# Branch B's output product in a conv-encoder step: three of four tile pairs as seven block products

## The chip, the cores and the metric

The kernel runs on one core of one Trainium2 chip. The metric is device time in microseconds (us), the median of the runs shown. One core has a matrix engine (PE, with its weight loads as PEld), a vector engine (DVE), a scalar engine (ACT), GpSimd (POOL) and SyncE (SP); the last three issue DMAs.

## The reference, cut to what matters

One layer of a streaming encoder on 576 token columns (512 of a prompt, 64 of a running stream), model width 1024, feed-forward width 2816:

```python
x = x + 0.5 * swiglu_ffn(rms_norm(x, ffn1_norm), ffn1_w_gate_up, ffn1_w_down)
h = rms_norm(x, mix_norm)
p = h @ w_in
...
y_a = (a_b * a_conv) @ w_a_out
...
b_act = jax.nn.silu(layer_norm(b_conv + conv_b_bias, conv_b_ln_g, conv_b_ln_b))
y_b = b_act @ w_b_out
merged = jax.nn.sigmoid(gate_a) * y_a + jax.nn.sigmoid(gate_b) * y_b
x = x + merged @ w_out
x = x + 0.5 * swiglu_ffn(rms_norm(x, ffn2_norm), ffn2_w_gate_up, ffn2_w_down)
```

A final norm and the convolutions' history rows follow. All data are float32. The change is in `y_b = b_act @ w_b_out` and in where `x` lies around it.

## The kernel before

**Layout.** Features lie on the 128 partitions and tokens along the row, so an activation is eight tiles of 128 x 576. The two halves of a tile's row (288 columns each) are two matmuls. The residual x lies in eight fixed tiles `X[j]` in SBUF.

**Products in parts.** Each weight block and each activation is split in a high part, rounded to the matmul's reduced float32, and the low part that is left; a product is high x high + high x low + low x high. A *plain* output tile (`product`, L430, with `mm`, L391) takes 8 row blocks of weights x 3 parts x 2 halves = 48 matmuls of 288 columns, in two weight *units* of four row blocks (24 matmuls each).

**Pairs in block form.** Most of the two feed-forwards' gate and up tiles go as `pair` (L773): two output tiles by two halves of the features by two halves of the tokens make a 2 x 2 block product, done as seven block products of sums instead of eight. Each block is 4 row blocks x 3 parts = 12 matmuls of 288 columns. The sums of weights (`s1` to `s4`) are made by DVE from four raw weight blocks; the sums of activations are four combinations per pair of tiles, made by `Forms.combine` (L570) with four half-width DVE operations and two ACT casts, and completed by `Forms.split` (L581) with two DVE subtractions. The seven results lie in PSUM and are combined by half-width DVE operations, after each block those that its result permits (`steps`).

**The weight stream** (`Stream`, L195) prepares units in one fixed order. A raw block (512 x 128, 256 KB) is loaded on SP's queue into one of 6 buffers, its high part is cast on ACT (`begin`, L257), and its low part is made in one of two ways: "dma" (ACT writes the negated high part, and a DMA issued by POOL accumulates the raw block onto it) or "dve" (`end`, L273, a subtraction on DVE). In a pair, sums are of the second kind, the blocks 1, 5 and 7, whose weights are raw blocks, of the first. Plain mixer units are all "dma". When PE's unit n is asked for (`get`, L298), `lead` (L287) first completes units up to n + `ahead` - 1, makes the sums of units up to n + `ahead` + 1, and begins units up to n + `ahead`; `ahead` is 6 (`AHEAD_UNITS`). Each unit has a home, the pool of its two buffers: "u" (8 buffers), "g" (8, shared with convolution tiles and branch B's gates) or "act" (44, shared with the split activations). Mixer units alternate between "u" and "act".

**Order of the work.** Every engine executes its instructions in the order in which the program writes them (`Ordered`, L71), so an ACT cast written behind an instruction that waits also waits. What `product` leaves to do with its result is written behind the next product's matmuls (`behind`, `take`, L421), and small DVE pieces queued in `work` are taken between products (`fill`, L417) by a planned cost.

**The stage around the change** (L1083 to L1141): eight rounds of branch A's gate `("p", 5, j)` and output product `("ya", j)`, whose gated results `M[j]` lie in four "act" and four "w" buffers; the layer norm's and the activation's pieces for branch B (`swish`, L1029), which give the eight split operands `BA`; eight tiles of branch B's gate `("p", 6, j)`; eight plain tiles of branch B's product, each with a scaling by the gate `SGB[j]`, an addition to `M[j]` and a split into `MS[j]`; and eight tiles of the output product, whose results are added to `X[j]`.

```python
for j in range(KT):
    ps = product(("yb", j), BA)
    dve.tensor_tensor(halves(SGB[j]), ps, halves(SGB[j]), op=ALU.mult)
    dve.tensor_tensor(M[j], M[j], SGB[j], op=ALU.add)
    MS.append(split(M[j]))
```

Of the kernel before, what the change touches and what calls it, by code (L numbers as in the profile page):

```python
# [1 line left out]

# [5 lines left out]
F32 = mybir.dt.float32  # L8
# [98 lines left out]
def tile_encoder_step(  # L107
# [19 lines left out]
    tmp = ctx.enter_context(tc.tile_pool(name="tmp", bufs=6))  # L127
    rpool = ctx.enter_context(tc.tile_pool(name="rpool", bufs=1))
    mmps = ctx.enter_context(tc.tile_pool(name="mmps", bufs=4, space=bass.MemoryType.PSUM))

# [6 lines left out]
    def atile(dt=F32, n=T):  # L137
        return act.tile([P, T], dt, tag="act", name=nm("act"))[:, :n]
# [56 lines left out]
    class Stream:  # L195
# [9 lines left out]

        def raw(self, w, row0, k, col0):
            ap = w[0, row0 : row0 + k * P, col0 : col0 + P].rearrange("(k p) n -> p k n", p=P)
            self.raws.append((ap, k))
            self.last.append({})
            return len(self.raws) - 1  # L210
# [97 lines left out]
    def home(other):  # L308

        homes[0] += 1  # L310
        return ("u", other)[homes[0] % 2]

    def plan_tile(name, w, row0, ks, col0, other, home_of=None, low="dma"):
        plan[name] = []
        for k in ks:
            r = ws.raw(w, row0, k, col0)
            plan[name].append(ws.unit(r, k, home_of or home(other), low))
            row0 += k * P
# [6 lines left out]
    def plan_pair(f, gu, i):  # L325

        a21, a22, a11, a12 = (
            ws.raw(gu, h * KU * P, KU, gu_col(part, i)) for part in "ug" for h in range(2)  # L330
        )
        s1, s2, s3, s4 = (f"{f}{i}s{n}" for n in range(1, 5))
        plan[f, "s", i] = [
            ws.unit(src, KU, home("g"), low, sums)
            for src, low, sums in (
                (a11, "dma", ((s1, (a21, a22)),)),
                (s2, "dve", ((s2, (s1, a11)),)),
                (s1, "dve", ()),
                (s3, "dve", ((s3, (a11, a21)),)),
                (a12, "dma", ()),  # L340
                (s4, "dve", ((s4, (s2, a12)),)),
                (a22, "dma", ()),
            )
        ]
# [24 lines left out]

    def plan_mixer(name, w, col):  # L370
        plan_tile(name, w, 0, (KU, KU), col, "act")

# [6 lines left out]
    for j in range(KT):  # L379
        plan_mixer(("p", 5, j), w_in, 5 * D + j * P)  # L380
        plan_mixer(("ya", j), w_a_out, j * P)
    for j in range(KT):
        plan_mixer(("p", 6, j), w_in, 6 * D + j * P)
    for j in range(KT):
        plan_mixer(("yb", j), w_b_out, j * P)
    for j in IN_TURN:
        plan_mixer(("o", j), w_out, j * P)
    plan_ffn("f2", ffn2_gu, ffn2_dn)
# [15 lines left out]
    def chunks(name):  # L404

        got = []
        for n in plan[name]:
            w = ws.get(n)
            got += [(w, kk) for kk in range(ws.units[n][1])]
        return got  # L410


# [145 lines left out]
    class Forms:  # L558

        def __init__(self, r_g):
            self.r_g, self.b, self.t, self.parts = r_g, {}, {}, {}
# [166 lines left out]
    def ffn(f, xg, sums, finish, forms, R=None, todo=()):  # L730
# [42 lines left out]
        def pair(i, hs, last):  # L773
# [21 lines left out]
            for n, xs in enumerate(bs):  # L795
                w = ws.get(plan[f, "s", i][n])
                q.append(bank()[:, :H])
                for k in range(KU):
                    (whi, wlo), (xh, xl) = w, xs[k]
                    for m, (l, r) in enumerate(((whi, xh), (whi, xl), (wlo, xh))):  # L800
                        pe.matmul(
                            q[n], l[:, k, :], r, start=k == m == 0, stop=k == KU - 1 and m == 2
                        )
                if n > 0:
                    steps[n - 1]()
                if rest:
                    rest.pop(0)()
# [197 lines left out]
    def b_of(j):  # L1005
# [9 lines left out]
        return then  # L1015

    for j in range(KT):
        for b, of in ((1, c_of), (2, cv_of), (0, b_of)):
            product(("p", b, j), xg, of(j))

    M, SGB, BA = [], [], []

# [6 lines left out]
    def swish(i, RL, sig={}):  # L1029
# [13 lines left out]
        if 0 <= j < KT:  # L1043
            BA[j] = (BA[j], low(sig[j], BA[j]))

    def ga_of(j):
# [5 lines left out]
    def ya_of(j):  # L1052
        def then(ps):
            m = atile() if j < 4 else wtile(n=T)
            dve.tensor_tensor(halves(m), ps, halves(gates.pop(j)), op=ALU.mult)
            M.append(m)
        return then
# [35 lines left out]
    while stage[0] < 4:  # L1093
        while work:
            work.pop(0)()
        advance()
    work.extend((lambda i=i: swish(i, RL)) for i in range(KT + 2))

# [11 lines left out]
    while work:  # L1110
        work.pop(0)()
    take()

    MS = []
    for j in range(KT):
        ps = product(("yb", j), BA)
        dve.tensor_tensor(halves(SGB[j]), ps, halves(SGB[j]), op=ALU.mult)
        dve.tensor_tensor(M[j], M[j], SGB[j], op=ALU.add)
        MS.append(split(M[j]))

    ss = Sum()
    xg = [None] * KT
    forms = Forms(R_N2)
    table(AF.Abs_reciprocal_sqrt)
    for n, j in enumerate(IN_TURN):
        ps = product(("o", j), MS)
        dve.tensor_tensor(halves(X[j]), ps, halves(X[j]), op=ALU.add)
        xg[j] = split_scaled(X[j], par(j, R_N2))
# [127 lines left out]
```

## Time and profile before

| | |
|---|---|
| median of 3 runs | 1299.93 us (1299.71 to 1300.36) |
| the profiled execution | 1300.08 us, its span 1298.3 us |
| matmuls | 9754, mean granted clock 0.998 |
| branch A's rounds, last output tile ends | 750.96 us from the span's start |
| branch B's gate product | 750.96 to 800.88 us |
| branch B's output product | 800.88 to 850.80 us |
| the mixer's output product | 850.80 to 900.72 us |

A row of a timeline gives start, length, engine, source line, operation, tiles written and read, shapes and count, and in brackets the engine's idle time before it and what ended it. As helpers record every operation, all rows bear line L83: what tells them apart is the tile names. "act", "u", "g" and "w" are buffer pools, "mm" is PSUM, "raw" an unsplit weight block. PE's rows overlap by the drain of each matmul, so the distance between two starts, and not a length, is what a matmul costs. A bracketed busy share is an average over stages; what a stage is worth is read from its own rows.

### The profile page before, as it was taken

Reading aid. Unit: us, or ns where it says so; the run is one execution under the profiler, and the core shown is the slowest. Engines: PE = TensorE matmul, PEld = TensorE weight load, DVE = VectorE, ACT = ScalarE, POOL = GpSimd, SP = SyncE. Lnnn points to the kernel's source line nnn. Section 1 sums busy time; section 2 is a strip of 40 time slices with the busy share of each in tenths; the row PEclk is TensorE's granted clock in tenths of the full one; section 3 lists DMA queues with packets and bytes.
Section 4 is the critical chain, followed back from the end, with each engine's and each line's share of the span. In section 5 each row is a group of like instructions: output and inputs, shape, how many; then the busy total and the mean of one; then the engine's idle time right before and its main releaser. Section 6 shows DMA issues by size and latency. Waiting matters only on the chain.

```text
span 1298.3 us, 25689 instructions
## 1 busy us (share of the span) xinstructions
PE 1286.2 (99%) x9754; PEld 1283.6 (99%) x9754; DVE 892.1 (69%) x1469; ACT 768.7 (59%) x1362; POOL 380.7 (29%) x481
## 2 busy tenths in 40 slices
PE   9999999999999999999999999999999999999997
PEld 9999999999999999999999999999999999999996
DVE  6848758748945999888885160336967848847955
ACT  7746646645677654555444674467665655654664
POOL 0042332232233454333321322222142242241231
PEclk9999999999999999999999999999999999999999
DMA  7397786896698898778875978776688697796784
GB/s 219 79 196 159 157 185 155 164 196 143 151 199 180 168 212 175 169 166 177 168 168 128 197 158 174 164 157 142 139 174 175 144 194 160 155 211 133 161 176 108
DMA packets 287516, 215.39 MB, mean 166 GB/s; under 512 B 15520, under 2 KB 250016, under 8 KB 287392
## 3 DMA queue, kind: packets, MB, share of 16 engines
q0 software_dynamic: 59184, 97.28, 45.7%
q1 hardware_dynamic: 226336, 115.49, 31.4%
q8 instruction: 77, 1.26, 0.4%
q10 hardware_dynamic: 1872, 0.97, 0.3%
q14 instruction: 47, 0.39, 0.1%
HBM read 113.81 MB, written 2.62 MB: 90 GB/s over the span
## 4 chain that ended last, share of the span: by engine, by line
PE 94%; issue 2%; DVE 2%; DMA 1%; ACT 1%; POOL 0%; DVEq 0%; POOLq 0%; ACTq 0%
PE mm L83 94%; DVE tmp L83 1%; DMA u<-raw 0%; DVE g L83 0%; ACT tmp L83 0%; DMA act<-raw 0%; DMA raw<-in_ffn_w_gate_up_dram 0%; DVE x L83 0%; ACT act L83 0%; DVE acc L83 0%; ACT r L83 0%; DVE act L83 0%; ACT w L83 0%; ACT L83 0%; DVEq L1246 0%
## 5 line engine op out<-in xcount | busy, mean ns | idle before, releaser
L83 PE MATMUL mm<-act,u 128*128 128x288 f32 x4686 | 661.1, 294 | 1.2 <-DMA u<-raw 1.2
L83 PEld LDWEIGHTS mm<-act,u 128*128 128x128 f32 x4686 | 631.1, 188 | 1.7 <-DMA u<-raw 1.7
L83 PE MATMUL mm<-act,g 128*128 128x288 f32 x2778 | 399.7, 294 | 0.5 <-DMA g<-raw 0.4
L83 PEld LDWEIGHTS mm<-act,g 128*128 128x128 f32 x2778 | 378.1, 188 | 0.9 <-DMA g<-raw 0.6
L83 PE MATMUL mm<-act,act 128*128 128x288 f32 (+2 forms) x2244 | 306.7, 293 | 0.2 <-DMA act<-raw 0.2
L83 PEld LDWEIGHTS mm<-act,act 128*128 128x128 f32 x2244 | 297.6, 188 | 0.4 <-DMA act<-raw 0.4
L83 POOL DMA_DIRECT2D u<-raw x199 | 173.9, 874 | 373.0 <-ACT u L83 306.3
L83 ACT CAST u<-raw 128x512 fp32r<-128x512 f32 (+2 forms) x203 | 116.2, 572 | 165.2 <-PE mm L83 122.3
L83 POOL DMA_DIRECT2D g<-raw x122 | 106.7, 875 | 310.2 <-ACT g L83 241.4
L83 DVE SCALAR_TENSOR_TENSOR w<-g,prm,w 128x606 f32<-128x606 f32 x232 | 179.3, 843 | 1.4 <-ACT w L83 1.4
L83 DVE TENSOR_TENSOR tmp<-mm,tmp 128x288 f32<-128x288 f32 (+1 forms) x239 | 107.7, 459 | 70.2 <-PE mm L83 52.1
L83 POOL DMA_DIRECT2D act<-raw x90 | 78.0, 866 | 199.1 <-ACT act L83 195.4
L83 ACT ACTIVATE u<-u 128x512 fp32r<-128x512 f32 (+2 forms) x199 | 117.9, 593 | 6.3
L83 ACT CAST g<-raw 128x512 fp32r<-128x512 f32 (+2 forms) x126 | 68.9, 547 | 39.2 <-DMA raw<-in_ffn_w_down_dram 14.5
L83 ACT CAST u<-w 128x512 fp32r<-128x512 f32 x79 | 48.9, 619 | 60.1 <-DVE w L83 51.4
L83 DVE SCALAR_TENSOR_TENSOR tmp<-mm,r 128x576 f32<-128x576 f32 x48 | 36.3, 756 | 68.2 <-PE mm L83 68.2
L83 ACT CAST g<-w 128x512 fp32r<-128x512 f32 x77 | 47.7, 619 | 57.6 <-DVE w L83 50.1
L83 ACT CAST act<-tmp 128x576 fp32r<-128x576 f32 x84 | 56.7, 675 | 40.8 <-DVE tmp L83 39.0
L83 DVE TENSOR_TENSOR act<-tmp,act 128x576 fp32r<-128x576 f32 x84 | 62.1, 754 | 18.8 <-ACT act L83 17.2
L83 ACT ACTIVATE g<-g 128x512 fp32r<-128x512 f32 (+2 forms) x122 | 69.2, 567 | 3.9
L83 DVE TENSOR_TENSOR w<-raw,raw 128x512 f32<-128x512 f32 x78 | 53.5, 686 | 15.9 <-DMA raw<-in_ffn_w_gate_up_dram 15.9
L83 ACT CAST act<-raw 128x512 fp32r<-128x512 f32 (+3 forms) x94 | 55.6, 592 | 10.3 <-PE mm L83 7.5
(88 smaller groups left out, 804.8 us busy)
## 6 DMA issues: line engine op xcount, KB each, us to landing
raw<-in_ffn_w_gate_up_dram SPq DMA_DIRECT2D x171, 256.0 KB, 3.4
u<-raw POOLq DMA_DIRECT2D x140, 256.0 KB, 4.1
raw<-in_w_in_dram SPq DMA_DIRECT2D x112, 256.0 KB, 3.6
act<-raw POOLq DMA_DIRECT2D x80, 256.0 KB, 4.2
raw<-in_ffn_w_down_dram SPq DMA_DIRECT2D x96, 192.0 KB, 3.6
g<-raw POOLq DMA_DIRECT2D x63, 256.0 KB, 3.9
u<-raw POOLq DMA_DIRECT2D x43, 192.0 KB, 4.4
g<-raw POOLq DMA_DIRECT2D x43, 192.0 KB, 4.5
```

The costliest lines, as they stand in the source:

```text
L83: return self.tc.keep_in_program_order(fn(*args, **kwargs))
```

## The change

Tiles 0 and 1 of branch B's output product stay plain. Tiles 2 to 7 become three pairs in block form, with a function `block` shared with the feed-forwards' `pair`. The activation sums are formed from the unsplit tiles `sig[j]` that `swish` leaves, for the first two pairs of tiles among `swish`'s pieces and for the last two behind the gate product. `M[j]` takes the place of `X[j]`; `X[j]` is stored to DRAM during the branch A input products and loaded back when `M[j]` is split. Look-ahead becomes 4 from the gate product on, 5 for the pairs and 6 again after them. Homes: three of four units in "u" for the gate product and the two plain tiles, a list for the pairs, "u" and "g" by turns for the output product. The splits of tiles 4 and 5 are put into the third pair, those of 6 and 7 behind it.

```diff
+            ap = rows[:, col0 : col0 + P].rearrange("(k a p) n -> a p k n", a=step, p=P)
+            self.raws.append((ap[row0 // P if step > 1 else 0], k))
...
+    few = cycle(("u", "u", "u", "act"))
     for j in range(KT):
-        plan_mixer(("p", 6, j), w_in, 6 * D + j * P)
-    for j in range(KT):
-        plan_mixer(("yb", j), w_b_out, j * P)
+        plan_mixer(("p", 6, j), w_in, 6 * D + j * P, few)
+    for j in range(2):
+        plan_mixer(("yb", j), w_b_out, j * P, few)
+    for i in range(1, KU):
+
+        plan_block(("yb", "s", i), [
+            ws.raw(w_b_out, h * P, KU, j * P, 2) for j in (2 * i + 1, 2 * i) for h in range(2)
+        ], ("u", "act", "u", "g", "u", "act", "u"))
     for j in IN_TURN:
-        plan_mixer(("o", j), w_out, j * P)
+        plan_tile(("o", j), w_out, 0, (KU, KU), j * P, "g")
...
+    def block(w, xs):
+
+        q = bank()[:, :H]
+        for k in range(KU):
+            (whi, wlo), (xh, xl) = w, xs[k]
+            for m, (l, r) in enumerate(((whi, xh), (whi, xl), (wlo, xh))):
+                pe.matmul(q, l[:, k, :], r, start=k == m == 0, stop=k == KU - 1 and m == 2)
+        return q
...
     for j in range(KT):
         for b, of in ((1, c_of), (2, cv_of), (0, b_of)):
             product(("p", b, j), xg, of(j))
-
-    M, SGB, BA = [], [], []
+        nc.sync.dma_start(kept[j], X[j])
+
+    M, SGB, BA = X, [], []
+    forms = Forms()
...
             BA[j] = (BA[j], low(sig[j], BA[j]))
+            forms.b.setdefault(j // 2, []).append(sig[j])
...
-            m = atile() if j < 4 else wtile(n=T)
-            dve.tensor_tensor(halves(m), ps, halves(gates.pop(j)), op=ALU.mult)
-            M.append(m)
+            dve.tensor_tensor(halves(M[j]), ps, halves(gates.pop(j)), op=ALU.mult)
...
-    work.extend((lambda i=i: swish(i, RL)) for i in range(KT + 2))
+    for i in range(KT + 2):
+        work.append(lambda i=i: swish(i, RL))
+
+        if i in (3, 5):
+            work.append(lambda p=(i - 3) // 2: forms.combine(p))
+        if i in (4, 6):
+            work.append(lambda p=(i - 4) // 2: forms.split(p))
+    ws.ahead = 4
...
+    for p in range(KU // 2, KU):
+        forms.combine(p)
     take()
-
-    MS = []
-    for j in range(KT):
+    for p in range(KU // 2, KU):
+        forms.split(p)
+
+    MS = [None] * KT
+
+    def back(*js):
+        for j in js:
+            nc.sync.dma_start(X[j], kept[j])
+
+    for j in range(2):
         ps = product(("yb", j), BA)
         dve.tensor_tensor(halves(SGB[j]), ps, halves(SGB[j]), op=ALU.mult)
         dve.tensor_tensor(M[j], M[j], SGB[j], op=ALU.add)
-        MS.append(split(M[j]))
-
+        MS[j] = split(M[j])
+
+    ws.ahead = 5
+    bs = forms.operands(BA[::2] + BA[1::2])
+    for i in range(1, KU):
+        j = 2 * i
+        c1, c2, qu, uu = (ttile() for _ in range(4))
+        q1, u2, u3, u4 = half(qu, 0), half(qu, 1), half(uu, 0), half(uu, 1)
+        q = []
+
+        def row(j, c):
+            dve.tensor_tensor(c, c, SGB[j], op=ALU.mult)
+            dve.tensor_tensor(M[j], M[j], c, op=ALU.add)
+            if j < 4:
+                MS[j] = split(M[j])
+
+        def second():
+            dve.tensor_tensor(u3, q[3], u2, op=ALU.add)
+            dve.tensor_tensor(half(c2, 1), u3, q[2], op=ALU.subtract)
+
+            if i == KU - 1:
+                MS[4], MS[5] = split(M[4]), split(M[5])
+
+        def first():
+            dve.tensor_tensor(half(c1, 1), q[5], u4, op=ALU.add)
+            row(j, c1)
+
+        steps = (
+            lambda: sca.copy(q1, q[0]),
+            lambda: dve.tensor_tensor(u2, q[1], q1, op=ALU.subtract),
+            lambda: dve.tensor_tensor(u4, q[2], u2, op=ALU.subtract),
+            second,
+            lambda: dve.tensor_tensor(half(c1, 0), q[4], q1, op=ALU.add),
+            first,
+        )
+        for n, xs in enumerate(bs):
+            q.append(block(ws.get(plan["yb", "s", i][n]), xs))
+            if n > 0:
+                steps[n - 1]()
+            if n == 2 and i < 3:
+                back(j - 2, j - 1)
+        dve.tensor_tensor(half(c2, 0), q[6], u3, op=ALU.add)
+        row(j + 1, c2)
+    spare.clear()
+    ws.ahead = AHEAD_UNITS
+    MS[6], MS[7] = split(M[6]), split(M[7])
+    back(4, 5)
...
     for n, j in enumerate(IN_TURN):
         ps = product(("o", j), MS)
+        if n == 0:
+            back(6, 7)
```

More of the change, by code (lines that the diff above doesn't have):

```diff
@@ L1 @@
+from collections.abc import Iterator
 from contextlib import ExitStack
+from itertools import cycle
 import concourse.bass as bass
@@ L128, in tile_encoder_step @@
     rpool = ctx.enter_context(tc.tile_pool(name="rpool", bufs=1))
+    dram = ctx.enter_context(tc.tile_pool(name="dram", bufs=1, space=bass.MemoryType.DRAM))
     mmps = ctx.enter_context(tc.tile_pool(name="mmps", bufs=4, space=bass.MemoryType.PSUM))
@@ L204, in __init__, with raw @@
             self.sums, self.eager = {}, False
-        def raw(self, w, row0, k, col0):
-            ap = w[0, row0 : row0 + k * P, col0 : col0 + P].rearrange("(k p) n -> p k n", p=P)
-            self.raws.append((ap, k))
+        def raw(self, w, row0, k, col0, step=1):
+            rows = w[0, row0 : row0 + k * P] if step == 1 else w[0]
+            ap = rows[:, col0 : col0 + P].rearrange("(k a p) n -> a p k n", a=step, p=P)
+            self.raws.append((ap[row0 // P if step > 1 else 0], k))
             self.last.append({})
@@ L316, in plan_tile @@
             r = ws.raw(w, row0, k, col0)
-            plan[name].append(ws.unit(r, k, home_of or home(other), low))
+            to = next(home_of) if isinstance(home_of, Iterator) else home_of or home(other)
+            plan[name].append(ws.unit(r, k, to, low))
             row0 += k * P
@@ L325, in plan_pair, with plan_block @@
     def plan_pair(f, gu, i):
-        a21, a22, a11, a12 = (
+        plan_block((f, "s", i), [
             ws.raw(gu, h * KU * P, KU, gu_col(part, i)) for part in "ug" for h in range(2)
[L331 to L335, printed above, removed]
+        ], [home("g") for _ in range(7)])
+    def plan_block(name, raws, homes):
+        a21, a22, a11, a12 = raws
+        s1, s2, s3, s4 = ((name, n) for n in range(1, 5))
+        plan[name] = [
+            ws.unit(src, KU, home, low, sums)
+            for home, (src, low, sums) in zip(homes, (
                 (a11, "dma", ((s1, (a21, a22)),)),
@@ L342, in plan_pair @@
                 (a22, "dma", ()),
-            )
+            ))
         ]
@@ L368, in tile_encoder_step, with plan_mixer @@
     plan_ffn("f1", ffn1_gu, ffn1_dn)
-    def plan_mixer(name, w, col):
-        plan_tile(name, w, 0, (KU, KU), col, "act")
+    def plan_mixer(name, w, col, home_of=None):
+        plan_tile(name, w, 0, (KU, KU), col, "act", home_of)
     for j in range(KT):
@@ L558, in tile_encoder_step, with __init__ @@
     class Forms:
-        def __init__(self, r_g):
+        def __init__(self, r_g=None):
             self.r_g, self.b, self.t, self.parts = r_g, {}, {}, {}
@@ L795, in pair @@
             for n, xs in enumerate(bs):
[L796 to L803, printed above, removed]
+                q.append(block(ws.get(plan[f, "s", i][n]), xs))
                 if n > 0:
@@ L1015, in b_of @@
         return then
+    kept = [
+        dram.tile([P, T], F32, tag=f"kept{j}", name=f"kept{j}") for j in range(KT)
+    ]
     for j in range(KT):
@@ L1118, in tile_encoder_step @@
         dve.tensor_tensor(M[j], M[j], SGB[j], op=ALU.add)
-        MS.append(split(M[j]))
+        MS[j] = split(M[j])
[39 more added lines that the diff above has]
+    back(4, 5)
+    ss = Sum()
+    xg = [None] * KT
+    forms = Forms(R_N2)
     ss = Sum()
```

## The prediction

> **What bounds the kernel now.** I read the page first, then the table of stretches for the stages around the change, then the timelines of the matrix engine (PE), the vector engine (DVE), the scalar engine (ACT) and GpSimd (POOL) there.
>
> ```profile
> span 1298.3 us, 25689 instructions
> PE 1286.2 (99%) x9754; PEld 1283.6 (99%) x9754; DVE 892.1 (69%) x1469; ACT 768.7 (59%) x1362; POOL 380.7 (29%) x481
> PE 94%; issue 2%; DVE 2%; DMA 1%; ACT 1%; POOL 0%; DVEq 0%; POOLq 0%; ACTq 0%
> ```
>
> PE is busy for 99% of the span and makes 94% of the chain that ended last: the time is the matmul count times their spacing, plus whatever makes PE wait. The profiled run took 1300.08 us, of which 1298.3 are its span; the median is 1299.93. I work out a difference and apply it to the median.
>
> ```profile
> 751.00:801.00 50.00, 50.00 (x386) 50.00 (x386) 21.81 (x33) 33.12 (x53) 12.90 (x15) 1.00 0.81 168
> 800.88:850.80 49.92, 49.92 (x386) 49.92 (x385) 15.92 (x21) 23.75 (x40) 13.75 (x16) 1.00 0.72 156
> 913.82:924.94 11.12, 11.12 (x87) 11.12 (x85) 9.33 (x16) 7.91 (x14) 2.50 (x3) 1.00 0.69 143
> ```
>
> Columns after the length: busy PE, weight loads, DVE, ACT, POOL, granted clock, DMA share. Row 1 is the gate product ahead of branch B's, row 2 the eight tiles of branch B's product itself, row 3 one pair of the second feed-forward, which has the form that the change introduces. PE never idles in any of them. DVE has two thirds of its time free in row 2, and only 1.8 of 11.12 us in row 3: that is what the change uses up.
>
> **The change part by part: PE.**
>
> ```profile
> 706.59 3.32 PE L83 MATMUL mm<-act,act 128*128 128x288 f32 x24
> 709.75 3.32 PE L83 MATMUL mm<-act,u 128*128 128x288 f32 x24
> ...
> 807.12 3.28 PE L83 MATMUL mm<-act,act 128*128 128x288 f32 x24
> ...
> 813.36 3.28 PE L83 MATMUL mm<-act,act 128*128 128x288 f32 x24
> ...
> 850.80 3.28 PE L83 MATMUL mm<-act,act 128*128 128x288 f32 x24
> ...
> 913.82 1.74 PE L83 MATMUL mm<-act,g 128*128 128x288 f32 x12
> 915.39 1.76 PE L83 MATMUL mm<-act,u 128*128 128x288 f32 x12
> ...
> 924.94 1.74 PE L83 MATMUL mm<-act,u 128*128 128x288 f32 x12
> ```
>
> Second tile 807.12, third 813.36: 6.24 us for 48 matmuls, 130 ns each. Six tiles take 37.44 us (813.36 to 850.80). A pair in block form takes 7 x 12 = 84 matmuls, from 913.82 to 924.94: 11.12 us, 1.59 per block. Three pairs: 33.36. Removed: **4.08 us**, if nothing waits.
>
> **DVE and ACT, first wait.** All weights become a high and a low part. A "dma" unit's low part is cast and negated on ACT, then accumulated by a DMA from POOL. Blocks 1, 5 and 7 of a pair are such units, the others subtract on DVE.
>
> ```profile
> 813.56 0.76 DVE L83 TENSOR_TENSOR w<-mm,w 128x576 f32<-128x576 f32 x1 [3.19 <-PE mm L83]
> 814.35 0.76 DVE L83 TENSOR_TENSOR act<-act,w 128x576 f32<-128x576 f32 x1
> 815.86 0.76 DVE L83 TENSOR_TENSOR act<-act,act 128x576 fp32r<-128x576 f32 x1 [0.74 <-ACT act L83]
> 815.14 0.68 ACT L83 CAST act<-act 128x576 fp32r<-128x576 f32 x1 [3.20 <-DVE act L83]
> 815.73 0.61 ACT L83 CAST act<-raw 128x512 fp32r<-128x512 f32 x1
> 816.37 0.63 ACT L83 ACTIVATE act<-act 128x512 fp32r<-128x512 f32 x1
> 816.91 0.60 ACT L83 CAST u<-raw 128x512 fp32r<-128x512 f32 x1
> 817.30 0.86 POOL L83 DMA_DIRECT2D act<-raw  x1 [4.19 <-ACT act L83]
> DMA to landing us min/median/max: 3.3/3.8/4.8
> DMA to landing us min/median/max: 3.8/4.1/4.7
> ```
>
> This is what follows the second tile today: PE ends at 813.36, DVE scales and adds, ACT casts the sum (815.14), and only then, in ACT's order, begins the next weights. The change keeps this order. With the look-ahead of 4 during the two plain tiles, weights are begun up to block 4 of the first pair; block 5 is begun at block 1's request, and so behind the cast at 815.14. Its accumulate starts at 817.30 and lands 4.1 us later (the second landing row, that of the "u" buffers, which block 5 uses): 821.4. PE wants it at the third matmul of block 5: 813.36 + 4 x 1.59 + 0.26 = 819.98. **PE waits 1.4 us** (0.6 to 2.1 with the landings' 3.3 to 4.8).
>
> **Second wait.** Spacings on DVE:
>
> ```profile
> 912.90 0.68 DVE L83 TENSOR_TENSOR w<-w,raw 128x512 f32<-128x512 f32 x1
> 913.68 0.62 ACT L83 CAST u<-w 128x512 fp32r<-128x512 f32 x1 [0.23 <-DVE w L83]
> 917.27 0.69 DVE L83 TENSOR_TENSOR u<-w,u 128x512 fp32r<-128x512 f32 x1
> 917.87 0.69 DVE L83 TENSOR_TENSOR w<-raw,raw 128x512 f32<-128x512 f32 x1
> 918.47 0.75 DVE L83 TENSOR_TENSOR tmp<-mm,r 128x576 f32<-128x576 f32 x1
> 919.14 0.68 DVE L83 TENSOR_TENSOR w<-w,raw 128x512 f32<-128x512 f32 x1
> ...
> 872.73 0.45 DVE L83 TENSOR_TENSOR tmp<-w 128x288 f32<-128x288 f32 x1
> 873.22 0.46 DVE L83 TENSOR_TENSOR tmp<-w,tmp 128x288 f32<-128x288 f32 x1
> 873.59 0.45 DVE L83 TENSOR_TENSOR tmp<-w,w 128x288 f32<-128x288 f32 x1
> ```
>
> From start to start a 512-wide operation costs 0.60, a 576-wide one 0.67 (0.79 where the next needs its result: 813.56 to 814.35), a half 0.37 (0.49 likewise). A pair needs 8 of 512 (four sums, four low parts, 4.8 us), 7 halves from PSUM (about 2.9) and, new against a feed-forward pair's, two products and two additions for the two rows (about 3.1); the first pair also splits both rows (two low parts, each behind an ACT cast: 815.86 less 814.35 = 1.51 from the addition, then 0.67). That is some 12 us in 11.1 us of PE, and the queue is already late at its start. In program order behind the low part at 815.86 stand ten 512-wide operations (for the first pair the fourth sum and the low parts of blocks 4 and 6, for the second its four sums and the low parts of blocks 2, 3 and 4), 6.0, and five halves, 2.1. A low part of a fresh sum also waits for the sum's cast: 0.68 for the sum, 0.10 + 0.62 for the cast (912.90 to 913.68 and its length), a signal; less the work that stands between, this leaves DVE idle for 0.8 at block 6 and 0.6 at the second pair's first sums. So 815.86 + 0.67 + 6.0 + 2.1 + 1.4 = 826.0 for the last half of row 1, where PE gave its data at about 813.36 + 6 x 1.59 + 1.4 = 824.3. Then row 1: half 0.49, product 0.79, addition to low part 1.51, low part 0.67: 829.5. Row 2: 0.49 + 0.79 + 0.79, so ACT may cast its sum at 831.6. Behind that cast in ACT's order stand the second pair's blocks 6 and 7: cast 0.59 later (815.14 to 815.73), the second 0.54 after (816.37 to 816.91, the spacing where nothing is waited for), then its negation 0.64 and the accumulate 0.93 later (815.73 to 816.37 to 817.30): accumulate at 834.3, landed 838.4. PE wants block 7 at 813.36 + 1.4 + 11.12 + 6 x 1.59 + 0.26 = 835.7. **PE waits 2.7 us.** The first wait cancels from the total, since this landing follows from DVE's chain alone: both together are 4.1 us (3.3 to 4.9 by the landings).
>
> The Trainium skill (VectorE: DVE Perf Modes, "The DRAIN you can't avoid") says that the next DVE operation does not start until the pipeline is empty (it excepts operations that nothing holds). The rows show starts 0.08 before the former's end; by the strict reading the 20 operations above would cost some 1.6 us more and the sum would be that much worse, an estimate from that page. For accumulates the landing rows say 3.8 and 4.1. The Trainium skill (DMA: Bandwidth & Descriptors, "Anatomy of one DMA") fits a GpSimd-issued DMA at 2.0 us plus bytes over 436 GB/s, an estimate of 2.6 us for 256 KB; the trace does not agree, and by the formula the change would keep about 1.6 us.
>
> **Third pair and the output product.** The second pair splits no row, so DVE there does 11 us in 11.1 plus the wait, and the third prepares almost no DVE weights (the output product's are "dma" units) and gets back its lag. Its end: half 0.49 more than today's chain (product 0.79, addition, cast, low part), so the last low part is ready about 4 us after the last block; the output product wants tile 7 of its eight operands after 36 matmuls, 4.7 us, and tile 8 at 5.5. Covered by about 1.5 us; that is what it costs if DVE is still later.
>
> **Forms, buffers, queues.** Sixteen extra halves, eight casts and eight low parts (16 x about 0.42 + 8 x 0.67 = 12 us on DVE) go into the gate product, where DVE has 28 of 50 us free, and the two plain tiles: hidden, at most delaying the sums, which is counted above. With three of four weight units in the 8 "u" buffers ACT waits for PE to free one, with 4 units of 3.12 us ahead against a chain of cast, negation and landing of about 6: covered by 6 us.
>
> ```profile
> L228 SPq DMA_DIRECT2D raw<-in_w_b_out_dram x16: 367/368/368, 770.9 to 817.0; - x16
> x<-in_x_dram SPq DMA_DIRECT2D x8, 288.0 KB, 5.3
> ```
>
> The residual makes 8 stores and 8 loads of 288 KB on SP, 0.37 us of issue each; the nearest landing is 5.3. The stores wait for nothing (X is final by then) and delay weight loads by 0.4 us under six units of look-ahead, 18 us. The loads stand on SP behind the split of their tile, and weight loads of the pair after next behind them, which are 10 us early; X is wanted at the ends of output tiles, the earliest 6 us into that product. I take nothing; the bound is one landing, 5.3 us, if a weight load were caught behind a late row, and below nothing is excluded, as no transfer goes away from PE's path.
>
> **PE's spacing** in the output product is 130 ns today, but the same form of product ran at 3.16 us for 24 (706.59 to 709.75), 132 ns. If the blocks leave PE in that state, 384 x 1.7 ns = 0.65 us more; I take none and keep it for the range.
>
> **Sum.** -4.08 + 1.4 + 2.7 = 0.0: **1299.9 us**; its own range by landings and spacing is 1299.1 to 1301.4. About 0.2% (2.6 us) is what a measurement can tell from no change.
>
> **The rivals.** *The second wait does not arise.* If DVE is on time at row 2 (PE's data at 825.9), its cast comes 3.5 us or more earlier and block 7's landing meets PE; only 1.4 is lost: 1299.93 - 4.08 + 1.4 = 1297.2. For it: the feed-forward pairs lose nothing with nearly the same DVE work. Against: they look 6 units ahead rather than 5, and begin with sums already made. 0.13. *Neither wait*: 1295.9. It needs accumulates that land in 2.7 us, under the least row, 3.3. 0.07. *The third pair waits too* (slower): the place is block 7 of the third pair, whose cast follows that pair's fourth sum on DVE. The same list, counted on from the end of row 2's split (833.0), puts that sum at 839.8, the accumulate at 842.6 and its landing at 846.7; PE wants it at 813.36 + 4.1 + 22.24 + 9.8 = 849.5. It decides once DVE is 2.8 us later than I count. A raw block of that pair caught behind two residual loads (2 x 0.37) and landing as late as x's 5.3 makes 6.0, less 2.8 is 3.2: 1303.1. Against: the second pair splits no row, and its raw buffers come free early. 0.08. My forecast keeps 0.72.
>
> **How the numbers follow.** Faster holds the first two rivals, 0.20; slower the third, 0.08; same 0.72. The range goes from 1296.6, which takes in the first rival and leaves out the second, to 1301.8, which takes in the forecast's own bounds and most of the way to the third.
>
> **What would show it.** PE's timeline should show two idles in the product, each ended by an accumulate into a "u" buffer: about 1.4 us at block 5 of the first pair and 2.7 at block 7 of the second, the output product starting within 1 us of 850.8. DVE should be near full from the second tile to the second pair. PE's matmuls should fall by 36. PE without idles there, an output product starting at about 847, or DVE with gaps in the first pair would prove me wrong; an idle ended by a raw load or by X would show that the residual's copies are not free.

## The result, and the profile after

The changed kernel takes 1304.31 us (median of 6 runs, 1303.57 to 1305.71), beside 1300.14 us (1299.62 to 1301.67) for the kernel before on the same chip: a ratio of 1.0034, 95% interval 1.0024 to 1.0044. The forecast was no change, in a range up to 1301.8; the kernel became slower by 0.34%, some 4.2 us. The profiled run of after took 1303.85 us.

The page first: matmuls have fallen by exactly the 36 forecast (9754 to 9718), yet the span is 3.7 us longer, and PE's share of the chain that ended last fell from 94 to 92%.

```profile
span 1302.0 us, 25764 instructions
PE 1284.8 (99%) x9718; PEld 1281.6 (98%) x9718; DVE 926.8 (71%) x1538; ACT 777.3 (60%) x1379; POOL 379.2 (29%) x478
PE 92%; DVE 2%; issue 2%; ACT 1%; DMA 1%; POOL 0%; DVEq 0%; POOLq 0%; ACTq 0%
```

So there is less work and more waiting. PE's timeline shows where (helpers record on L85 now; the stages here start about 0.94 us earlier than in the run of before, so compare lengths, not starts):

```profile
812.42 1.74 PE L85 MATMUL mm<-act,u 128*128 128x288 f32 x12
...
818.76 0.43 PE L85 MATMUL mm<-act,u 128*128 128x288 f32 x2
820.03 1.59 PE L85 MATMUL mm<-act,u 128*128 128x288 f32 x10 [0.84 <-DMA u<-raw]
...
823.06 1.75 PE L85 MATMUL mm<-act,u 128*128 128x288 f32 x12
829.01 3.22 PE L85 MATMUL mm<-act,u 128*128 128x288 f32 x12 [4.20 <-DVE tmp L85]
832.02 2.67 PE L85 MATMUL mm<-act,act 128*128 128x288 f32 x12
834.53 1.75 PE L85 MATMUL mm<-act,u 128*128 128x288 f32 x12
...
840.88 3.34 PE L85 MATMUL mm<-act,u 128*128 128x288 f32 x24
844.06 1.76 PE L85 MATMUL mm<-act,act 128*128 128x288 f32 x12
...
853.60 3.32 PE L85 MATMUL mm<-act,g 128*128 128x288 f32 x24
```

The first idle, at the third matmul of block 5 of the first pair, is the forecast one, ended by the forecast accumulate. The second is not: 4.20 us **between** the first and the second pair, ended by DVE and not by a DMA. And at block 7 of the second pair, where 2.7 us had been forecast, there is none: the row at 840.88 holds that block and the next in one piece.

The table of stretches adds what a timeline hides, the granted clock of PE. It is the third figure from the end; the two behind it are the DMA share and GB/s.

```profile
812.42:824.66 12.24, 11.40 (x86) 11.09 (x84) 10.19 (x18) 7.84 (x14) 3.04 (x4) 1.00 0.72 154
824.66:829.01 4.35, 0.15 (x2) 0.03 (x1) 3.51 (x7) 0.67 (x1) 0.41 (x1) 0.79 0.95 226
829.01:834.53 5.52, 5.52 (x24) 5.52 (x25) 4.06 (x6) 3.78 (x7) 0.86 (x1) 0.54 0.54 155
834.53:840.88 6.35, 6.35 (x50) 6.35 (x49) 3.48 (x7) 3.12 (x5) 0.86 (x1) 1.00 0.83 179
840.88:853.60 12.72, 12.72 (x98) 12.72 (x97) 10.61 (x20) 9.05 (x16) 5.19 (x7) 1.00 0.75 147
853.60:904.16 50.56, 50.56 (x386) 50.56 (x385) 27.39 (x45) 38.11 (x62) 13.77 (x16) 1.00 0.95 213
```

In the third stretch PE is busy throughout, and its 24 matmuls take 5.52 us where the 24 from 840.88 to 844.06, of the same form, take 3.18 (1.59 a block, as do the eight blocks of the fifth stretch): the clock stands at 0.54, and 2.34 us go without any idle to show for them. The output product takes 50.56 us instead of 49.92.

The account, from the start of the first pair to the end of the output product: three pairs at 33.3 us would save 4.1 on the 37.44 of six tiles. Lost are 1.1 at block 5 of the first pair, 4.35 between the pairs, 2.34 by the clock and 0.64 in the output product, 8.4 in all; 8.4 - 4.1 = +4.3, beside +4.2 of the medians.

What ended the 4.20 us is read on DVE:

```profile
827.74 0.76 DVE L85 TENSOR_TENSOR act<-x,act 128x576 fp32r<-128x576 f32 x1 [0.74 <-ACT act L85]
828.41 0.45 DVE L85 TENSOR_TENSOR tmp<-mm,tmp 128x288 f32<-128x288 f32 x1
```

The half at 828.41 reads the result of block 7 of the first pair (`half(c2, 0)`, written behind the loop over the blocks); it ends at 828.86, and PE goes on at 829.01. DVE is late there, as the prediction had counted: that half starts 16.0 us behind the first pair's start (828.41 less 812.42), and the prediction's list has it at 16.1 (829.5 less 813.36). Why should PE need it? Results are handed out like this (L160):

```python
def bank():

    if not spare:
        t = psum2()
        spare.extend((t[:, 0, :], t[:, 1, :]))
    return spare.pop(0)
```

One PSUM tile has two banks, and two blocks in a row share it. A pair has seven blocks, an odd number: block 7 of the first pair and block 1 of the second share a tile. **The theory**: as the read of block 7 is written ahead of the next pair's block 1, and the wait hangs on the tile as a whole, PE may not write the second bank until DVE has read the first; the clock then falls because of the idle. In the feed-forwards the tiles are shared in the same way, but there the read of block 7 is put behind the next pair's block 1 (`rest`), so nothing is to be waited for. **The rivals**: DVE's lateness holds PE in another way, by weights or buffers; the clock falls for another reason; the residual's copies cost; the output product's new homes make its longer spacing.

### The profile page after: what moved, and what is told of

Same layout as the page of the kernel before. It is cut to its first block, busy times and chain, and to the rows that moved or that the text cites. A ratio compares the mean times of both kernels' runs of the same rounds, so it can differ in the third digit from the quotient of the medians.

```text
span 1302.0 us, 25764 instructions
## 1 busy us (share of the span) xinstructions
PE 1284.8 (99%) x9718; PEld 1281.6 (98%) x9718; DVE 926.8 (71%) x1538; ACT 777.3 (60%) x1379; POOL 379.2 (29%) x478
## 4 chain that ended last, share of the span: by engine, by line
PE 92%; DVE 2%; issue 2%; ACT 1%; DMA 1%; POOL 0%; DVEq 0%; POOLq 0%; ACTq 0%
PE mm L85 92%; DVE tmp L85 1%; DMA u<-raw 1%; DVE g L85 0%; DVE act L85 0%; DVE x L85 0%; ACT tmp L85 0%; ACT act L85 0%; DMA raw<-in_ffn_w_gate_up_dram 0%; DVE w L85 0%; ACT u L85 0%; DVE acc L85 0%; DVE u L85 0%; ACT r L85 0%; ACT w L85 0%
## 5 line engine op out<-in xcount | busy, mean ns | idle before, releaser
L85 PE MATMUL mm<-act,u 128*128 128x288 f32 x4806 | 679.1, 294 | 6.4 <-DVE tmp L85 4.2
L85 PEld LDWEIGHTS mm<-act,u 128*128 128x128 f32 x4806 | 648.3, 188 | 7.9 <-issue 4.4
L85 PE MATMUL mm<-act,g 128*128 128x288 f32 x3006 | 431.2, 294 | 0.4 <-DMA g<-raw 0.4
L85 PEld LDWEIGHTS mm<-act,g 128*128 128x128 f32 x3006 | 408.5, 188 | 0.9 <-DMA g<-raw 0.6
L85 POOL DMA_DIRECT2D u<-raw x207 | 182.3, 881 | 455.0 <-ACT u L85 371.6
L85 PE MATMUL mm<-act,act 128*128 128x288 f32 (+2 forms) x1860 | 255.6, 294 | 0.0
L85 PEld LDWEIGHTS mm<-act,act 128*128 128x128 f32 x1860 | 248.2, 188 | 0.0
L85 ACT CAST u<-raw 128x512 fp32r<-128x512 f32 (+2 forms) x211 | 121.2, 574 | 175.2 <-PE mm L85 133.8
L85 POOL DMA_DIRECT2D g<-raw x130 | 115.1, 887 | 324.3 <-ACT g L85 277.4
L85 DVE SCALAR_TENSOR_TENSOR w<-g,prm,w 128x606 f32<-128x606 f32 x232 | 179.2, 842 | 1.4 <-ACT w L85 1.4
L85 DVE TENSOR_TENSOR tmp<-mm,tmp 128x288 f32<-128x288 f32 (+1 forms) x257 | 115.4, 458 | 74.7 <-PE mm L85 56.9
L85 ACT ACTIVATE u<-u 128x512 fp32r<-128x512 f32 (+2 forms) x207 | 123.0, 594 | 6.6
L85 ACT CAST g<-raw 128x512 fp32r<-128x512 f32 (+2 forms) x134 | 73.7, 550 | 35.0 <-DMA raw<-in_ffn_w_down_dram 18.8
L85 POOL DMA_DIRECT2D act<-raw x71 | 61.8, 871 | 109.4 <-ACT act L85 108.8
L85 DVE SCALAR_TENSOR_TENSOR tmp<-mm,r 128x576 f32<-128x576 f32 x48 | 36.3, 756 | 74.2 <-PE mm L85 74.1
L85 ACT CAST u<-w 128x512 fp32r<-128x512 f32 x82 | 50.7, 619 | 63.2 <-DVE w L85 58.0
L85 ACT CAST g<-w 128x512 fp32r<-128x512 f32 x80 | 49.5, 619 | 63.8 <-DVE w L85 57.6
L85 ACT CAST act<-tmp 128x576 fp32r<-128x576 f32 x92 | 61.9, 675 | 41.9 <-DVE tmp L85 40.2
L85 DVE TENSOR_TENSOR act<-tmp,act 128x576 fp32r<-128x576 f32 x92 | 67.5, 754 | 18.7 <-ACT act L85 17.2
L85 ACT ACTIVATE g<-g 128x512 fp32r<-128x512 f32 (+2 forms) x130 | 74.2, 571 | 4.1
L85 DVE TENSOR_TENSOR w<-raw,raw 128x512 f32<-128x512 f32 x84 | 57.5, 685 | 23.0 <-DMA raw<-in_ffn_w_gate_up_dram 11.9
L85 DVE TENSOR_TENSOR w<-w,raw 128x512 f32<-128x512 f32 x84 | 57.5, 684 | 3.8 <-DMA raw<-in_ffn_w_gate_up_dram 3.5
```

Source lines behind the costliest of these rows:

```text
L85: return self.tc.keep_in_program_order(fn(*args, **kwargs))
```

## The experiments

**A fresh tile for each pair.**

```diff
         q = []
+        spare.clear()
 
         def row(j, c):
```

> Every pair begins with a fresh two-bank PSUM tile, so that block 1 of the second pair no longer takes the second half of the tile whose first half is block 7 of the first. Theory (shared tile): the 4.20 us idle ahead of the second pair goes, and with it the loss of clock behind it (24 matmuls in 5.5 us instead of 3.2, 2.3 us). PE then reaches block 7 of the second pair at about 834.5 of the changed kernel's time scale, while its cast stands behind the cast of row 2's sum at 830.48 as before, so that its accumulate lands at about 837.3: the wait of the prediction appears, 2.8 us (2.0 to 3.6). Time: 1304.3 - 4.2 - 2.3 + 2.8 = 1300.6. Rival (DVE's lateness itself holds PE back, by weights or by buffers, and the PSUM tile is only where the trace puts it): an idle of about 4 us stays at the start of the second pair, 1304.3.

Measured: 1300.22 us beside 1299.74 of before, ratio 1.0002 (0.9993 to 1.0011). PE's timeline:

```profile
819.26 0.43 PE L85 MATMUL mm<-act,u 128*128 128x288 f32 x2
820.53 1.59 PE L85 MATMUL mm<-act,u 128*128 128x288 f32 x10 [0.84 <-DMA u<-raw]
...
823.56 3.75 PE L85 MATMUL mm<-act,u 128*128 128x288 f32 x24
827.15 1.77 PE L85 MATMUL mm<-act,act 128*128 128x288 f32 x12
...
835.09 0.42 PE L85 MATMUL mm<-act,u 128*128 128x288 f32 x2
837.24 3.19 PE L85 MATMUL mm<-act,u 128*128 128x288 f32 x22 [1.72 <-DMA u<-raw]
840.26 1.76 PE L85 MATMUL mm<-act,act 128*128 128x288 f32 x12
```

```profile
828.93 0.45 DVE L85 TENSOR_TENSOR tmp<-mm,tmp 128x288 f32<-128x288 f32 x1
```

The idle between the pairs is gone, and 24 matmuls run across that place in 3.59 us (823.56 to 827.15). The wait of the prediction has come up where it had been forecast, at the third matmul of block 7, ended by the accumulate: 1.72 us of idle. One line of code returns about the whole loss (from 1.0034 to 1.0002), and the kernel stands where the prediction had put it. The rival on DVE's lateness is out: DVE is as late here, as its read of block 7 again starts 16.0 us behind the first pair's start (828.93 less 812.93).

**Work in the idle.** Thirty more matmuls, whose result nobody reads, ahead of the second pair.

```diff
         q = []
+        if i == 2:
+            t = psum2()
+            for n in range(30):
+                pe.matmul(t[:, 0, :H], ones_r, half(BA[0][0], 0), start=True, stop=True)
```

> The changed kernel, with 30 further matmuls of 288 columns (of resident operands, their result read by nobody) ahead of block 1 of the second pair: they fill 3.9 of the 4.20 us that PE stands idle there. Theory (the idle costs twice, by its length and by the clock that falls behind it): the granted clock stays near 1.00 in the stretch that followed the idle (0.54 before), its 24 matmuls take 3.2 us instead of 5.5, no other wait comes up at block 7 of that pair (wanted at about 838.8, landed at about 837.3), time 1304.3 - 2.3 = 1302.0. Rival (the clock falls for another reason, such as the load on the other engines): 24 matmuls still take 5.5 us, 1304.3.

```profile
825.13 4.12 PE L85 MATMUL mm<-act,ones_r 128*128 128x288 f32 x30
829.51 1.82 PE L85 MATMUL mm<-act,u 128*128 128x288 f32 x12 [0.27 <-DVE tmp L85]
```

```profile
829.51:832.77 3.26, 3.26 (x25) 3.26 (x25) 2.49 (x4) 1.75 (x4) 0.00 (x0) 1.00 0.58 176
```

PE still waits for the same DVE operation, for 0.27 us, but now the two blocks behind it take 3.26 us at a clock of 1.00, instead of 5.52 at 0.54. From the first pair's start to the output product the profile shows 38.91 us instead of 41.18: 2.27 less, as expected for the clock alone. So matmuls that nobody needs make this stage shorter, by way of the clock. The whole time is 1302.72 beside 1299.74, ratio 1.0025 (1.0013 to 1.0038). That is 1.2 us better than the changed kernel's ratio, but the two intervals overlap: the times alone show neither the 2.3 us nor, for certain, a gain. The mean granted clock over whole runs was 0.994 to 0.997 in the six of the changed kernel and 0.997 to 0.998 in these eleven.

**The tiles shifted by one half.**

```diff
     bs = forms.operands(BA[::2] + BA[1::2])
+    bank()
```

> One half of a PSUM tile is drawn ahead of the pairs, so that blocks 6 and 7 of the first pair share a tile, and it is block 7 of the second pair and block 1 of the third that do. Theory (shared tile): the idle at the start of the second pair goes; block 7 of the second pair waits for its accumulate, 2.8 us (2.0 to 3.6); and block 1 of the third pair now waits for DVE, which in the changed kernel read block 7 of the second pair 3.8 us after PE had finished it (844.64 against 840.88): 3 to 5 us of idle, with up to 2.3 us of lost clock behind it. Time 1304.3 - 6.5 + 2.8 + 3 to 7.3 = 1303.6 to 1307.9. Rival (DVE's lateness at the second pair is what holds PE): the idle stays at the start of the second pair and none appears at the third, 1304.3.

Measured: 1305.96 us beside 1299.74, ratio 1.0051 (1.0038 to 1.0063). PE's timeline, the stretch behind its idle, and the operation of DVE that ends the idle:

```profile
836.85 1.60 PE L85 MATMUL mm<-act,u 128*128 128x288 f32 x10 [1.48 <-DMA u<-raw]
841.87 3.15 PE L85 MATMUL mm<-act,u 128*128 128x288 f32 x12 [3.42 <-DVE tmp L85]
```

```profile
841.87:844.86 2.99, 2.99 (x12) 2.99 (x13) 2.01 (x3) 0.00 (x0) 0.57 (x1) 0.51 0.68 123
```

```profile
841.27 0.45 DVE L85 TENSOR_TENSOR tmp<-mm,tmp 128x288 f32<-128x288 f32 x1
```

The idle has moved with the sharing, from the second pair to the third (3.42 us; block 1 behind it at a clock of 0.51: 2.99 us instead of 1.59), and at block 7 of the second pair the accumulate is waited for. With the first experiment this shows that the shared tile makes the wait.

An unread first bank alone does not hold PE. The kernel before shows it behind the first pair of its second feed-forward, where block 7 and the next pair's block 1 share a tile as well: that block 1 starts at 924.94, right behind block 7 and without a wait, and DVE reads block 7 only 4.71 us later.

```profile
929.65 0.45 DVE L83 TENSOR_TENSOR tmp<-mm,tmp 128x288 f32<-128x288 f32 x1
```

DVE is later there than in the changed kernel, where it reads block 7 some 3.75 us behind its end (828.41 less 824.66). What differs is the place of the read in the program, behind the write (`rest`) and not ahead of it. Whether the chip could write one bank in the same moment in which the other is read, no row here shows.

**The residual's copies alone**, in the kernel before with its eight plain tiles.

```diff
             product(("p", b, j), xg, of(j))
+        nc.sync.dma_start(kept[j], X[j])
...
-    M, SGB, BA = [], [], []
+    M, SGB, BA = X, [], []
...
         MS.append(split(M[j]))
+        if j % 2:
+            for k in (j - 1, j):
+                nc.sync.dma_start(X[k], kept[k])
```

> The kernel before, its eight plain tiles kept, with the part of the change that stores the residual to DRAM, lets branch A's output take its place and loads it again. Theory: these 16 transfers of 288 KB are hidden, as the prediction took them: the time of the kernel before, 1300.1, within 0.2%. Rival (they take bandwidth or the SP queue from the weight loads): PE shows idles ended by raw loads, and up to 2 us more.

Measured: 1300.03 us beside 1299.74, ratio 1.0000 (0.9992 to 1.0009). The copies are hidden there. In the changed kernel's profile, too, no idle of PE is ended by the load of a raw block or of X.

**Look-ahead 5 one tile earlier**, with the fresh tile per pair.

```diff
     for j in range(2):
+        if j:
+            ws.ahead = 5
         ps = product(("yb", j), BA)
```

> The kernel with a fresh PSUM tile per pair, and the look-ahead of 5 set one plain tile earlier, so that the weights of block 5 of the first pair are begun at the head of the second plain tile and no longer behind the cast of its sum. The first wait (0.84 us ahead of ten matmuls of block 5) should go. What the prediction held of the total: the second wait's landing follows from DVE's chain alone, so PE only arrives 1.0 us earlier at block 7 of the second pair and waits 1.0 longer (2.7 instead of 1.72): 1300.2, no change. Rival (DVE's chain gains too, since the sums and low parts of the first pair are now asked for one tile earlier, ahead of the work of the second plain tile's sum): the second wait stays at 1.7 to 2.0 or shrinks, and the time falls by about 1.0 to 1299.2.

```profile
813.33 1.74 PE L85 MATMUL mm<-act,u 128*128 128x288 f32 x12
...
833.97 0.42 PE L85 MATMUL mm<-act,u 128*128 128x288 f32 x2
836.29 4.71 PE L85 MATMUL mm<-act,u 128*128 128x288 f32 x22 [1.91 <-DMA u<-raw]
```

```profile
832.83 0.86 POOL L85 DMA_DIRECT2D u<-raw  x1 [8.25 <-ACT tmp L85]
```

Measured: 1297.85 us beside 1299.48, ratio 0.9991 (0.9982 to 1.0000). The first wait is gone, and the second is not longer by what the first had been: counted from the first pair's start its accumulate lands at 22.96 us (836.29 less 813.33) instead of 24.31 (837.24 less 812.93), 1.35 us sooner. The work ahead of it gained as well, so the rival was right. The profiled run is the longest of the 11 (1300.84; the lowest 1297.51), and its rows show a part of the reason: behind 1.91 us of idle the clock fell, and 22 matmuls took 4.55 us, where with the fresh tile alone they took 3.02 (837.24 to 840.26).

```profile
836.29:840.84 4.55, 4.54 (x22) 0.62 0.94 225
840.84:850.38 9.54, 9.54 (x75) 1.00 0.91 176
```

**Row 2 later.** With that and a look-ahead of 6 in the pairs, the last half and `row(j + 1, c2)` of the first two pairs are written behind block 2 of the next.

```diff
-    ws.ahead = 5
+    ws.ahead = 6
...
+    rest = []
...
-        c1, c2, qu, uu = (ttile() for _ in range(4))
+        qu, c1, uu, c2 = (ttile() for _ in range(4))
...
+            if n == 1 and rest:
+                rest.pop()()
...
-        dve.tensor_tensor(half(c2, 0), q[6], u3, op=ALU.add)
-        row(j + 1, c2)
+        def last(row=row, j=j, q=q, u3=u3, c2=c2):
+            dve.tensor_tensor(half(c2, 0), q[6], u3, op=ALU.add)
+            row(j + 1, c2)
+
+        if i < KU - 1:
+            rest.append(last)
+        else:
+            last()
```

> As the one before, with a look-ahead of 6 in the pairs as well, and the last half and row 2's work (product, addition, split) of the first and second pair put behind block 2 of the next pair instead of at the pair's end. The weights of block 7 of the second pair are then begun ahead of the cast of row 2's sum and not behind it, which is the cause that the theory gives for the second wait. Expected: no idle of PE of more than 0.5 us in the product, pairs of 11.1 us each, the output product at about 1.0 + 1.9 + 0.4 = 3.3 us earlier than with the PSUM tile alone; DVE's work on row 2 is only moved, and its lag at the third pair might show as up to 0.7 us of waits at tiles 7 and 8 of the first output product. Time 1300.2 - 3.3 = 1296.9 (to 1297.6). Rival (DVE itself has too much work in the pairs, so that whatever is put later is missing later): the same 2 to 3 us come back at the third pair or in the output product, 1299 to 1300.

```profile
812.85:847.25 34.40, 34.05 (x254) 33.45 (x253) 30.07 (x54) 21.88 (x40) 10.32 (x12) 1.00 0.86 189
847.25:900.86 53.61, 52.23 (x388) 51.78 (x387) 27.84 (x45) 39.36 (x64) 13.76 (x16) 1.00 0.91 207
```

Measured: 1297.53 us beside 1299.48, ratio 0.9984 (0.9975 to 0.9993), faster than before, and so than the changed kernel. The three pairs take 34.40 us with 0.35 of idle (36.87 with the fresh tile alone, 812.93 to 849.80). Here the order on ACT and the look-ahead were changed together; the next run changes the order alone. In the profiled run, again the longest of its 11 (1300.08), the output product gives 3.0 us back. Its waits are at the last two operands, tiles 7 and 8, and ACT shows their source:

```profile
853.14 0.40 PE L85 MATMUL mm<-act,u 128*128 128x288 f32 x1 [0.99 <-ACT act L85]
853.94 1.75 PE L85 MATMUL mm<-act,u 128*128 128x288 f32 x11 [0.39 <-DVE act L85]
```

```profile
851.25 0.62 ACT L85 CAST u<-raw 128x512 fp32r<-128x512 f32 x1 [2.60 <-DMA raw<-in_w_out_dram]
...
852.44 1.23 ACT L85 CAST act<-x 128x576 fp32r<-128x576 f32 x2
```

The casts of the last two rows stand in ACT's order behind a weight whose raw block is late. These waits are 1.4 of the 3.0 us; some 0.9 more come from a third spacing of the matmuls behind them, 134.4 ns at a clock of 1.00 (336 matmuls in 45.17 us, 855.52 to 900.69).

**Row 2 of the first pair alone**, and the look-ahead 5 in the pairs; the edit against the kernel just told:

```diff
-    ws.ahead = 6
+    ws.ahead = 5
...
-        if i < KU - 1:
+        if i == 1:
             rest.append(last)
```

> As the kernel with the earlier look-ahead of 5 and a fresh PSUM tile per pair, but with the last half and row 2's work of the first pair alone put behind block 2 of the second pair (the second pair keeps its end, the look-ahead stays 5). If the order on ACT makes the second wait, this alone removes it (1.91 us in that kernel), and since row 2 of the second pair has no cast, moving it as well was of no use: the output product starts 1.9 us earlier than there, and has no waits at its tiles 7 and 8 (1.4 us where the look-ahead was 6 and both rows moved): time 1297.85 - 1.9 = 1296.0 (to 1297.0). Rival (DMA engines at 99% busy over the pairs, with landings of 5.6 to 6.8 us, are what makes weights late): 1 to 2 us of waits remain, 1297.5.

```profile
835.12 3.41 PE L85 MATMUL mm<-act,u 128*128 128x288 f32 x22 [0.62 <-DMA u<-raw]
...
847.91:898.47 50.56, 50.56 (x386) 50.56 (x385) 26.61 (x44) 37.79 (x62) 13.79 (x16) 1.00 0.96 216
```

```profile
829.35 0.86 POOL L85 DMA_DIRECT2D u<-raw  x1 [4.79 <-ACT tmp L85]
```

Measured: 1299.06 us beside 1299.51, ratio 0.9990 (0.9981 to 0.9999), a miss by 2 to 3 us. The output product has no idle, as expected. ACT's order did delay the weights of block 7: the accumulate is now issued 16.04 us behind the first pair's start (829.35 less 813.31) instead of 19.50 (832.83 less 813.33). But of these 3.5 us PE gets only 1.3, its wait falling from 1.91 to 0.62 us, as the accumulate lands after 5.77 us instead of 3.46 (after 6.50 in the kernel just told, 827.86 to 834.36). So landings as long as the rival's came too. Its reason did not show: the DMA share from issue to landing is 0.69 here and 0.85 in the profile with the quick landing. What makes it land late stays open.

From the first pair's start to the output product this profile has 34.60 us (813.31 to 847.91), 2.8 less than before's 37.44; with the 0.64 lost in the output product 2.2 should remain, and the times show 1.3, with an interval of 0.1 to 2.5. One profile is not enough here. The run with four more matmuls behind these same pairs, told next, has 35.90 us for them (811.99 to 847.89), with 0.34 us of idle at block 1 of the second pair and 1.66 at block 1 of the third:

```profile
836.93 1.58 PE L85 MATMUL mm<-act,u 128*128 128x288 f32 x10 [1.66 <-DMA u<-raw]
```

So 2.0 us of waits for accumulates remain there, as the rival had it. The interval overlaps with those of the two kernels above: which of the three is best, these runs do not tell.

**The spacing in the output product**, in four kernels: before with the homes of after, the fresh-tile kernel with the homes of before, and four more matmuls with unread results ahead of the output product, in the kernel just told and in the one before.

```diff
-        plan_mixer(("o", j), w_out, j * P)
+        plan_tile(("o", j), w_out, 0, (KU, KU), j * P, "g")
```

```diff
+    t = psum2()
+    for n in range(4):
+        pe.matmul(t[:, 0, :H], ones_r, half(BA[0][0], 0), start=True, stop=True)
```

> The kernel before, with the output product's weights in the buffers named g, as the change has them, instead of u and act in turn; nothing else. The output product took 50.56 us in the changed kernel and 49.92 before, with 386 matmuls in both (131.7 and 130.0 ns each). If the buffers make the difference: 50.56 here. If the blocks ahead leave PE in the longer spacing: 49.92.

> The kernel with a fresh PSUM tile per pair, and the output product's weights in u and act in turn, as before the change. If the buffers make the longer spacing: 49.92 us for the output product. If the blocks ahead of it do: 50.56.

> The one before with four further matmuls of 288 columns (result unread) ahead of the output product. In the kernel before, PE's spacing changes at each group of four matmuls with ones: 130.0 ns up to 693.42, 131.7 behind it, 130.0 again behind those at 719.23. If the spacing is a phase of the instruction stream that four matmuls shift, the output product's 384 matmuls go from 131.7 back to 130.0 ns: 49.92 us instead of 50.56, for 4 x 0.13 = 0.52 us of extra matmuls, -0.1 us in all. Rival (the blocks ahead, not the count, set it): 50.56 and +0.5 us.

> The kernel before with the same four further matmuls ahead of its output product. If four matmuls shift the phase: the output product goes from 49.92 to 50.56 us there, without any block ahead of it. Rival: 49.92.

The output product in these four, in that order:

```profile
849.72:899.64 49.92, 49.92 (x386) 49.92 (x385) 25.29 (x41) 36.12 (x59) 12.06 (x14) 1.00 0.75 157
```

```profile
850.07:900.62 50.55, 50.55 (x386) 50.55 (x385) 27.39 (x45) 38.10 (x62) 13.74 (x16) 1.00 0.94 214
```

```profile
848.41:898.97 50.56, 50.56 (x386) 50.56 (x385) 26.99 (x44) 37.78 (x62) 13.24 (x16) 1.00 0.95 212
```

```profile
850.98:901.50 50.52, 50.52 (x386) 50.52 (x385) 25.01 (x41) 36.14 (x59) 12.06 (x14) 1.00 0.75 159
```

The homes are not it: before keeps 49.92 with those of after, and the changed kernel keeps 50.55 with those of before. Nor does it take a block product: four plain matmuls ahead are enough to bring the kernel before to 50.52. But four more did not bring the changed kernel back (its time 1299.50 beside 1299.51, ratio 0.9997, 0.9988 to 1.0005). So what has gone before sets the spacing, but not simply in steps of four matmuls, as had been supposed; the rule stays open.

## Why the prediction was wrong, point by point

- **Matmuls, -4.08 us: right.** 36 fewer, and blocks at 1.59 us.
- **First wait, 1.4 us: right in place and mechanism; it cost 1.1.** In the fresh-tile kernel block 5's accumulate is issued at the forecast moment, 3.94 us behind the second tile's end, but lands 3.7 us later (816.87 to 820.53) instead of the 4.1 assumed.

```profile
816.87 0.86 POOL L85 DMA_DIRECT2D u<-raw  x1 [13.24 <-ACT u L85]
...
833.68 0.86 POOL L85 DMA_DIRECT2D u<-raw  x1 [8.11 <-ACT tmp L85]
```

- **Second wait, 2.7 us: right only once the tile is not shared.** There block 7's accumulate is issued 20.75 us behind the first pair's start (833.68 less 812.93); the prediction had 20.94 (834.3 less 813.36). It lands after 3.56 us, and PE loses 2.0 at that block (835.09 to 840.26 less two blocks of 1.59). The long addition of DVE's and ACT's operations held within 0.2 us; the landing, 3.56 instead of 4.1, made most of the difference. By the Trainium skill (VectorE: DVE Perf Modes, "The DRAIN you can't avoid"), as the prediction read it strictly, that issue would have come 1.6 us later; it did not.
- **"The first wait cancels from the total": wrong.** Removing it brought the second landing 1.35 us forward.
- **"Buffers": the step that failed.** Under forms, buffers and queues the prediction costed the "u" buffers and the raw blocks, and put the wait for PSUM at nothing without a reason, though it had DVE read block 7's half only after 829.5. Its own numbers held the loss: the half ends 0.49 later, at 830.0, where it let PE finish the pair at 813.36 + 1.4 + 11.12 = 825.9, a gap of 4.1 us. Measured: 4.20. It took a late DVE to cost only what stands behind it on ACT, and it took a pair's 11.12 us from the feed-forwards, where the read of block 7 is written behind the next block 1. PE's timeline refutes the first, and the fresh tile and the shift show that the shared tile is the reason.
- **The clock: not thought of.** Behind the idle of 4.20 us another 2.34 us were lost. Together they took the second wait away, since PE came to block 7 only after its weights.
- **The residual's copies, taken as nothing: right**, 1.0000 (0.9992 to 1.0009) in the kernel before.
- **Spacing, taken as zero and kept for the range: wrong by 0.64 us**, in the direction named.
- **The rivals.** The slower one, at the third pair, did not come; no rival named the start of a pair. Without the shared tile the forecast "no change" would have held (1.0002), but in part by luck: the two waits were 1.0 us smaller than stated (1.1 and 2.0 instead of 1.4 and 2.7), and two terms put at nothing made up for it, 0.4 at the second pair's block 1 (3.59 less 3.18) and 0.64 in the output product.

## What to carry to other kernels

When an engine is forecast to run late, list everything that it is to free, PSUM tiles too, and not only what stands behind it on the other engines; where results are handed out in halves of a tile, check at each seam, above all with an odd number of results, whose read stands in the program ahead of the next write to that tile. An idle of PE of some microseconds can cost more than its length (here those of 1.91 us and above did), so look at the granted clock in the stretch behind it. In an order written out by hand, a look-ahead begun one tile sooner and a row's cast written behind the next weights took 1.0 to 2.5 us out of the three pairs (36.87 to 35.90, 34.60 and 34.40 in the profiles).

## What the runs showed of the hardware

**The clock behind an idle.** PE's idles of 0.62, 0.84, 1.66 and 1.72 us left the clock at 1.00 in the next stretch or block. Behind 1.91 us it was 0.62 over 4.55 us, behind 3.42 it was 0.51 over 2.99 us, behind 4.20 it was 0.54 over 5.52 us; then it was back at 1.00. The Trainium skill (TensorE: Matmul & The Clock Gate, "HAM oscillation — how this bites in real kernels") warns of gaps over some 3.4 us. The two long ones agree; the loss behind 1.91 us does not, and here the measurement decides. Each of these is one profile. Whether such an idle also spreads the runs of one kernel (1297.51 to 1300.84 with the earlier look-ahead) was not tried, and the kernel with row 2 later spreads more (1294.75 to 1300.08), while the longest idle in the product in its profile is 0.99 us.

**The spacing of the matmuls.** The 384 matmuls of the output product take 130.0 or 131.7 ns each, by what has gone before and not by which buffers they read; four matmuls change it in one kernel and not in another, and in one profile 134.4 ns came up behind waits.

**The landing of an accumulate.** Two of 256 KB for the same block landed 3.46 us after their issue in one profile and 5.77 in another, at a DMA share of 0.85 and 0.69; what makes the difference is not shown.
